# Gate and up projections of four FFNs: one 512 wide product with the high part of a weight block over both parts of the input, then a 256 wide one with its low part

## The chip, the cores and the metric

One core of a Trainium2 chip runs one program. The metric is device time in microseconds (us) from one launch to its end. Engines are named as the profile names them: PE multiplies matrices (PEld is its loading of weights), DVE, ACT and POOL work on tiles in SBUF and PSUM, SP issues most DMAs.

## The reference, cut to what matters

A decoder trunk of two layers over 256 tokens of width 1024, all in float32. Each layer has two half-step FFNs around a token mixer: a gated linear recurrence in the first, attention in the second. So there are four FFNs, and each of them computes

```
def swiglu(x, w_gate, w_up, w_down):            # x 256x1024, w_gate and w_up 1024x2816, w_down 2816x1024
    return (jax.nn.silu(x @ w_gate) * (x @ w_up)) @ w_down
h = h + 0.5 * rms_norm(swiglu(rms_norm(h, g_pre), ...), g_post)
```

The change concerns `x @ w_gate` and `x @ w_up`.

## The kernel before, in words

**Split operands.** PE multiplies in a format that holds fewer bits than float32 (fp32r). So each weight tile `raw` (128 x 1024, 512 KB, loaded by SP) is split: ACT writes the rounded copy `whi` (L175), DVE the rest `wlo = raw - whi` (L176). The normed input is kept in the same way, turned, in `xall` (128 x 8 x 2 x 256): for each of 8 blocks of 128 features, 256 columns of the high part (`xhi`) and right behind them 256 columns of the low part (`xlo`). A product `w * x` is the sum of three: high times high, high times low, low times high.

**Two ways to project.** `mm3` (L181 to L185) keeps a block of the *input* still in PE and streams 512 weight columns; three products per block. `mmj` (L195 to L200) keeps a *weight* block (128 x 128) still and streams 256 tokens:

```
def mmj(ps, wh, wl, k, first, last):
    nc.tensor.matmul(ps, wh, xhi[:, k, :], start=first, stop=False)     # L198
    nc.tensor.matmul(ps, wh, xlo[:, k, :], start=False, stop=False)     # L199
    nc.tensor.matmul(ps, wl, xhi[:, k, :], start=False, stop=last)      # L200
```

The first two use the same weights, but each product loads its own. The result comes out turned (features in partitions, tokens in columns), as the down projection wants its still operand.

**An FFN** (`ffn_items`, L479) covers the 2816 hidden columns in five tiles of 512 and one of 256. The first tile of three of the four FFNs goes by `mm3` (gate, then up), the others by `mmj`: `tile_items` (L535) for 512 columns of the gate, then 512 of up; `last_items` (L558) for 256 of each. Such a *group* is four weight tiles, each with 2 x 4 blocks of 128 x 128, so 32 calls of `mmj`. Over all FFNs these are 38 groups, 152 weight tiles, 1216 calls, 3648 products. A group writes two PSUM banks of 512 columns, two blocks in each. At its end `gate_rows` (L518: DVE scales by the row of reciprocal norms `rrow`, ACT applies SiLU) or `up_rows` (L525: DVE multiplies with the gate, ACT makes `hhi`, DVE `hlo`) reads each of the two banks. Then comes the down projection (`row_items`, L440) by `mm3` with 512 wide products.

**PSUM** has 8 banks. Before, four rotate as `mm` (sums), two as `gt` (turning of the stream `h`), two as `tr` (other transpositions).

**Order.** PE's order is written out by hand: `run_ffn` (L606) goes through the items, `slot` does one item and calls `tick`, and `tick` places small work that was deferred by a number of ticks, such as transpositions (`hidden_T` L506, `rstd_rows` L256, `rg_params` L670, which turns the parameters of the recurrence once, in the first FFN). The other engines' orders come from a scheduler. Raw tiles have 5 buffers (`RAW`), split ones 9 (`WB`); a split is placed by `prepare_next` when its buffer is free and its load is estimated to have landed.

Of the kernel before, what the change touches and what calls it, by code (L numbers as in the profile page):

```python
# [16 lines left out]
P = 128  # L17
# [27 lines left out]
def trunk_kernel(ctx: ExitStack, tc: tile.TileContext, A: dict, out: bass.AP):  # L45
# [12 lines left out]
    def nm(s):  # L58
        uid[0] += 1
        return f"{s}_{uid[0]}"  # L60

    def mmbank():
        return psum.tile([P, 512], F32, tag="mm", name=nm("mm"), bufs=4)

    def gtbank():
        return psum.tile([P, 512], F32, tag="gt", name=nm("gt"), bufs=2)

    def trbank():
        return psum.tile([P, 512], F32, tag="tr", name=nm("tr"), bufs=2)

# [123 lines left out]

    def mmj(ps, wh, wl, k, first, last):  # L195

        tensor_work(3 * S)
        nc.tensor.matmul(ps, wh, xhi[:, k, :], start=first, stop=False)  # L198
        nc.tensor.matmul(ps, wh, xlo[:, k, :], start=False, stop=False)  # L199
        nc.tensor.matmul(ps, wl, xhi[:, k, :], start=False, stop=last)  # L200

# [54 lines left out]
    def rstd_rows():  # L256

        tp = trbank()
# [124 lines left out]
    def proj_items(w, c0, nn, get_x, post, nk=8):  # L383
# [4 lines left out]
        for k0 in range(0, nk, kper):  # L388
# [8 lines left out]
            def work(t, u, k0=k0, kn=kn, i=len(items)):  # L397
# [12 lines left out]
                if k0 + kn == nk:  # L410
                    post(t, acc[t][:, :nn])
            if not items:
# [27 lines left out]
    def row_items(w, widths, get_x, post, rows=2):  # L440
# [6 lines left out]
        for k, kp in enumerate(widths):  # L447
# [3 lines left out]
            def work(t, u, k=k):  # L451
# [13 lines left out]
                if k == nk - 1:  # L465
                    post(t, acc[t])
            items.append((prep, work))
            r0 += kp
# [10 lines left out]
    def ffn_items(pool_of, wg, wu, wd, post_g, next_dests, last=False, normed=False, lead=1):  # L479
# [9 lines left out]

        def gate_tile():  # L490
            return pool_of().tile([P, 512], F32, tag="sil", name=nm("sil"), bufs=2)

        def prod_tile():
            return pool_of().tile([P, 8 * HA], F32, tag="prod", name=nm("prod"), bufs=2)[:, :512]

        def post_gate(t, ps):
            s = sil[t] = gate_tile()
            nc.scalar.activation(s, ps, AF.Silu, scale=rs[t][:, 0:1])

        def post_up(c0):  # L500
            def f(t, ps):
                pr = prod_tile()
                nc.vector.tensor_tensor(pr, ps, sil[t], ALU.mult)
                defer(HT, lambda: hidden_T(pr, t))

            def hidden_T(pr, t):  # L506
                hh, hl = hid_tiles()
                tp = trbank()
                for j in range(4):
                    nc.tensor.transpose(tp[:, j * P:(j + 1) * P], pr[:, j * P:(j + 1) * P], ident)  # L510
                k0 = c0 // P
                hv = hh[:, t, k0:k0 + 4, :].rearrange("p a b -> p (a b)")
                lv = hl[:, t, k0:k0 + 4, :].rearrange("p a b -> p (a b)")
                nc.scalar.activation(hv, tp, AF.Copy)
                nc.vector.tensor_tensor(lv, tp, hv.bitcast(F32), ALU.subtract)
            return f

        def gate_rows(n, ps):  # L518
            s = sil["j", n] = gate_tile()
            v = s.rearrange("p (a b) -> p a b", a=2)  # L520
            nc.vector.tensor_tensor(v, ps.rearrange("p (a b) -> p a b", a=2),
                                    rcp["v"].unsqueeze(1).to_broadcast([P, 2, S]), ALU.mult)
            nc.scalar.activation(s, s, AF.Silu)

        def up_rows(n, ps, k0):  # L525
            hh, hl = hid_tiles()
            pr = prod_tile()
            nc.vector.tensor_tensor(pr, ps, sil["j", n], ALU.mult)
            pv = pr.rearrange("p (a t b) -> p a t b", a=2, t=2)
            hv = hh[:, :, k0:k0 + 2, :].rearrange("p t a b -> p a t b")  # L530
            lv = hl[:, :, k0:k0 + 2, :].rearrange("p t a b -> p a t b")
            nc.scalar.activation(hv, pv, AF.Copy)
            nc.vector.tensor_tensor(lv, pv, hv.bitcast(F32), ALU.subtract)

        def tile_items(w, c0, post):  # L535
            acc = {}

            for k0 in range(0, 8, 2):
                def prep(k0=k0):
# [3 lines left out]
                def work(t, u, k0=k0):  # L543
                    if k0 == 0:
                        acc["b"] = [mmbank(), mmbank()]
                    for j in range(2):
                        for b in range(4):
                            o = j * 512 + b * P
                            mmj(acc["b"][b // 2][:, (b % 2) * S:(b % 2 + 1) * S], u.hi[:, o:o + P], u.lo[:, o:o + P],
                                k0 + j, k0 + j + b % 2 == 0, k0 + j == 7 and b % 2 == 1)  # L550
                        if j == 0:
                            tick()
                    if k0 == 6:
                        for n in range(2):
                            post(n, acc["b"][n])
                items.append((prep, work))

        def last_items(c0):  # L558
            acc = {}

            for k0 in range(0, 8, 2):
# [7 lines left out]
                def work(t, u, k0=k0):  # L569
                    if k0 == 0:  # L570
                        acc["b"] = [mmbank(), mmbank()]
                    for j in range(2):
                        for b in range(4):
                            o = j * 512 + b * P
                            mmj(acc["b"][b // 2][:, (b % 2) * S:(b % 2 + 1) * S], u.hi[:, o:o + P], u.lo[:, o:o + P],
                                k0 + j, k0 + j + b % 2 == 0, k0 + j == 7 and b % 2 == 1)
                        if j == 0:
                            tick()
                    if k0 == 6:
                        gate_rows(0, acc["b"][0])  # L580
                        up_rows(0, acc["b"][1], c0 // P)
                items.append((prep, work))

        i0 = len(items)
        for i in range(5):
# [84 lines left out]
    def rg_params():  # L670
        tp = trbank()
        nc.tensor.transpose(tp[:RT, :NP], prow, ident[:NP, :NP])
# [33 lines left out]
    def add_gate_unit(g, k0, kn):  # L706
# [5 lines left out]
        def work(t, u):  # L712
# [6 lines left out]
            if k0 + kn == 8:  # L719
                if (g, t) not in ((0, 1), (2, 0)):  # L720
                    for gg, tt_ in {(1, 1): [(0, 1)], (2, 1): [(2, 0)]}.get((g, t), []) + [(g, t)]:
                        n = GCOLS[gg][1]
                        tok = toks[(gg, tt_)] = pools["r"].tile([P, 4 * RT], F32, tag="tok", name=nm("tok"), bufs=4)
                        nc.scalar.activation(tok[:, :n], gacc[(gg, tt_)][:, :n], AF.Gelu_apprx_tanh)
        rg[f"g{sum(n[0] == 'g' and n[1] != 'w' for n in rg)}"] = len(items)
        items.append((prep, work))
# [35 lines left out]
    def conv(p, ps):  # L762
# [9 lines left out]
        def taps(j, i):  # L772
            for k in (2, 1, 0):
                s = 3 - k
                nc.vector.scalar_tensor_tensor(xc[:w, j, s:], ps[:w, j * S:(j + 1) * S - s],
                                               par[:w, k * NRT + i:k * NRT + i + 1], xc[:w, j, s:], ALU.mult, ALU.add)

        first = [(1.25, ("c", p), lambda j=j, i=i: taps(j, i)) for j, i in enumerate(tl)]
# [79 lines left out]
    def batch(g):  # L858
# [20 lines left out]
        def gate_T(t):  # L879
            tok = toks[(g, t)]  # L880
            tp = tps[t] = trbank()
            for j in range(len(pairs) * 2 if g < 2 else 3):
# [3 lines left out]
        def product(t):  # L886
# [4 lines left out]
            for (a, b, w) in parts_of(g):  # L891
                tp = tps[t][:w, a * P:b * P].rearrange("p (a b) -> p a b", a=b - a)
                nc.vector.tensor_tensor(y[:w, a:b, :], tp, tt[g][:w, a:b, t * P:(t + 1) * P], ALU.mult)
                nc.scalar.activation(yy[g][0][:w, t, a:b, :], y[:w, a:b, :], AF.Copy)

        def low(t):
# [82 lines left out]
    def heads_T(pool, ps, t, n, scale, cols, dst):  # L979

        tok = pool.tile([P, 8, HA], F32, tag="prod", name=nm("htok"), bufs=2)
        nc.vector.tensor_scalar(tok[:, :, :HD], ps.rearrange("p (a b) -> p a b", a=8), rs[t][:, 0:1], scale,
# [7 lines left out]
        def turn(b):  # L990
            tp = trbank()
            for j in range(4):
# [41 lines left out]
    def v_items(c0, n, extra):  # L1034
# [3 lines left out]
        for k0 in range(0, 8, 2):  # L1038
# [9 lines left out]
            def work(t, u, k0=k0):  # L1048
# [6 lines left out]
                if k0 == 6:  # L1055
                    if extra:
                        post_f(t, ps[:, n:])
                    nc.scalar.activation(kv["v"][t][:, c0:c0 + n], ps[:, :n], AF.Copy, scale=rs[t][:, 0:1])
            items.append((prep, work))

# [20 lines left out]
    def attention(t):  # L1081
# [32 lines left out]
        def values(hg):  # L1114
# [8 lines left out]
            if hds[-1] % 8 == 7:  # L1123
                nc.vector.reciprocal(sm, sm)
                ot = box["ot", hds[-1] // 8] = ap.tile([P, 8, HD], F32, tag="ot", name=nm("ot"), bufs=2)
                nc.vector.tensor_tensor(ot, po.rearrange("p (a b) -> p a b", a=8),
                                        sm.unsqueeze(2).to_broadcast([P, 8, HD]), ALU.mult)

        def output(b):
# [198 lines left out]
```

## Time and profile before

| | before |
|---|---|
| median of 3 runs | 1019.05 us (1018.81 to 1019.17) |
| the profiled execution | 1018.94 us |
| its span, first to last instruction | 1017.2 us |
| PE products, all | 6518 |
| of them 256 wide by `mmj` | 3 x 1216 |
| granted PE clock | 0.998 |

A time is 1.7 us longer than the span of the same execution (1018.94 against 1017.2). Products are pipelined: a product's shown duration includes the time in which it drains, while the next one already streams. So what a product costs in a row of products is the distance from its start to the next one's start, which the timeline shows.

### The profile page before, as it was taken

Reading aid. Unit: us, or ns where it says so; the run is one execution under the profiler, and the core shown is the slowest. Engines: PE = TensorE matmul, PEld = TensorE weight load, DVE = VectorE, ACT = ScalarE, POOL = GpSimd, SP = SyncE. Lnnn points to the kernel's source line nnn. Section 1 sums busy time; section 2 is a strip of 40 time slices with the busy share of each in tenths; the row PEclk is TensorE's granted clock in tenths of the full one; section 3 lists DMA queues with packets and bytes.
Section 4 is the critical chain, followed back from the end, with each engine's and each line's share of the span. In section 5 each row is a group of like instructions: output and inputs, shape, how many; then the busy total and the mean of one; then the engine's idle time right before and its main releaser. Section 6 shows DMA issues by size and latency. Waiting matters only on the chain.

```text
span 1017.2 us, 16436 instructions
## 1 busy us (share of the span) xinstructions
PE 1004.2 (99%) x6518; PEld 915.0 (90%) x6518; DVE 628.3 (62%) x777; ACT 533.9 (52%) x734; POOL 52.7 (5%) x113
## 2 busy tenths in 40 slices
PE   8999999999999999999999999999999999999997
PEld 5999998889988999998898999998888889999885
DVE  5866554668997655554695555654477476556442
ACT  5645434559986544443565444443467565444331
POOL 2500000000003000000110000000020010000000
PEclk9999999999999999999999999999999999999999
DMA  6886646565336766556376666664555067665441
GB/s 231 284 257 198 192 160 187 164 183 151 122 99 226 229 186 186 187 151 180 116 242 221 191 181 180 185 183 164 165 167 166 1 189 247 186 183 182 155 125 41
DMA packets 91875, 179.07 MB, mean 176 GB/s; under 512 B 11790, under 2 KB 31318, under 8 KB 91798
## 3 DMA queue, kind: packets, MB, share of 16 engines
q1 hardware_dynamic: 90550, 176.89, 56.1%
q8 instruction: 51, 0.84, 0.3%
q10 hardware_dynamic: 608, 1.06, 0.3%
q0 software_dynamic: 640, 0.07, 0.1%
q14 instruction: 26, 0.21, 0.1%
HBM read 176.95 MB, written 1.05 MB: 175 GB/s over the span
## 4 chain that ended last, share of the span: by engine, by line
PE 90%; ACT 4%; DVE 4%; issue 2%; POOL 1%; DVEq 0%; POOLq 0%; ACTq 0%
PE mm L198 14%; PE mm L200 14%; PE mm L199 14%; PE mm L185 13%; PE mm L184 13%; PE mm L183 13%; PE gt L815 1%; DVE wlo L176 1%; PE mm L190 1%; PE mm L191 1%; PE mm L192 1%; PE gt L1094 1%; PE mm L1121 1%; ACT junk L213 1%; PE gt L222 1%
## 5 line engine op out<-in xcount | busy, mean ns | idle before, releaser
L176 DVE TENSOR_TENSOR wlo<-raw,whi 128x1024 fp32r<-128x1024 f32 (+4 forms) x329 | 395.1, 1207 | 297.2 <-ACT whi L175 295.4
L175 ACT ACTIVATE whi<-raw 128x1024 fp32r<-128x1024 f32 (+4 forms) x329 | 342.6, 1046 | 373.8 <-PE mm L199 207.9
L198 PE MATMUL mm<-xall,whi 128*128 128x256 f32 x1216 | 344.7, 283 | 0.0
L200 PE MATMUL mm<-xall,wlo 128*128 128x256 f32 x1216 | 344.1, 283 | 0.0
L199 PE MATMUL mm<-xall,whi 128*128 128x256 f32 x1216 | 344.1, 283 | 0.0
L198 PEld LDWEIGHTS mm<-xall,whi 128*128 128x128 f32 x1216 | 233.4, 192 | 0.2
L199 PEld LDWEIGHTS mm<-xall,whi 128*128 128x128 f32 x1216 | 233.4, 192 | 0.2
L200 PEld LDWEIGHTS mm<-xall,wlo 128*128 128x128 f32 x1216 | 233.4, 192 | 0.0
L183 PE MATMUL mm<-whi,hhi 128*128 128x512 f32 (+2 forms) x432 | 166.1, 384 | 0.0
L185 PE MATMUL mm<-whi,hlo 128*128 128x512 f32 (+2 forms) x432 | 165.0, 382 | 0.0
L184 PE MATMUL mm<-wlo,hhi 128*128 128x512 f32 (+2 forms) x432 | 164.9, 382 | 0.0
L185 PEld LDWEIGHTS mm<-whi,hlo 128*128 128x128 f32 x432 | 81.1, 188 | 15.0
L184 PEld LDWEIGHTS mm<-wlo,hhi 128*128 128x128 f32 x432 | 81.2, 188 | 14.7
L183 PEld LDWEIGHTS mm<-whi,hhi 128*128 128x128 f32 x432 | 81.2, 188 | 14.6
L183 PE MATMUL mm<-whi,xall 128*128 128x512 f32 (+2 forms) x168 | 67.1, 400 | 0.1
L184 PE MATMUL mm<-wlo,xall 128*128 128x512 f32 (+2 forms) x168 | 65.0, 387 | 0.4 <-DVE wlo L1191 0.2
L185 PE MATMUL mm<-whi,xall 128*128 128x512 f32 (+2 forms) x168 | 64.8, 386 | 0.1
L206 POOL TENSOR_SCALAR nv<-ss 128x1 f32<-128x1 f32 x24 | 10.9, 453 | 789.7 <-ACT junk L213 789.5
L184 PEld LDWEIGHTS mm<-wlo,xall 128*128 128x128 f32 x168 | 31.7, 188 | 7.4 <-DVE wlo L176 1.2
L185 PEld LDWEIGHTS mm<-whi,xall 128*128 128x128 f32 x168 | 31.6, 188 | 7.0 <-DVE xall L236 1.1
L183 PEld LDWEIGHTS mm<-whi,xall 128*128 128x128 f32 x168 | 31.6, 188 | 5.7 <-ACT xall L231 0.5
L277 DVE SCALAR_TENSOR_TENSOR t<-mm,rstd,gb 128x512 f32<-128x512 f32 x16 | 11.9, 749 | 26.7 <-ACT junk L213 26.7
(188 smaller groups left out, 938.9 us busy)
## 6 DMA issues: line engine op xcount, KB each, us to landing
raw<-in_ffn_w_down_dram SPq DMA_DIRECT2D x88, 512.0 KB
raw<-in_ffn_w_up_dram SPq DMA_DIRECT2D x80, 512.0 KB
raw<-in_ffn_w_gate_dram SPq DMA_DIRECT2D x79, 512.0 KB
raw<-in_rg_w_in_dram SPq DMA_DIRECT2D x20, 504.0 KB
raw<-in_rg_w_out_dram SPq DMA_DIRECT2D x10, 504.0 KB
raw<-in_ffn_w_gate_dram SPq DMA_DIRECT2D x18, 256.0 KB
raw<-in_ffn_w_up_dram SPq DMA_DIRECT2D x16, 256.0 KB
raw<-in_w_kv_dram SPq DMA_DIRECT2D x8, 512.0 KB
```

The costliest lines, as they stand in the source:

```text
L175: nc.scalar.activation(hi[:parts, c:c + m], rawv[:, c:c + m], AF.Copy)
L176: nc.vector.tensor_tensor(lo[:parts, c:c + m], rawv[:, c:c + m], hi[:parts, c:c + m].bitcast(F32), ALU.subtract)
L183: nc.tensor.matmul(ps, xh, wh, start=first, stop=False)
L184: nc.tensor.matmul(ps, xh, wl, start=False, stop=False)
L185: nc.tensor.matmul(ps, xl, wh, start=False, stop=last)
L190: nc.tensor.matmul(ps, wh, xh, start=first, stop=False)
L191: nc.tensor.matmul(ps, wh, xl, start=False, stop=False)
L198: nc.tensor.matmul(ps, wh, xhi[:, k, :], start=first, stop=False)
L199: nc.tensor.matmul(ps, wh, xlo[:, k, :], start=False, stop=False)
L200: nc.tensor.matmul(ps, wl, xhi[:, k, :], start=False, stop=last)
L206: nc.gpsimd.tensor_scalar(v, ss[:, 0:1], ss[:, 1:2] if n == 2 else 0.0, D * EPS * f * f, ALU.add, ALU.add)
L277: nc.vector.scalar_tensor_tensor(t1[n], pf[n], r_in, gb[:, n * 512:(n + 1) * 512], ALU.mult, ALU.mult)
```

## The change

`mmj` now takes two neighbouring blocks. For each it issues one 512 wide product of `wh` with both input parts, which lie side by side in `xall`, and after both of these the two 256 wide products of `wl` with the high part. The sums high times high and low times high stand in columns 0 to 255 of a bank, high times low in columns 256 to 511. So each block has a bank of its own, and a group four banks instead of two; the two halves are added when the bank is read out (`total`: ACT copies the second halves of all banks of a group to SBUF, DVE adds the first halves).

All 8 banks become one tile `pall`, handed out by `bank`. Gate groups and `last_items` use banks 4 to 7, up groups banks 0 to 3; while banks are in such use (`lent`), the small transpositions take one of the others (`sparebank`). `gate_rows` and `up_rows` do a whole group (1024 columns) in one instruction where there were two of 512, and their buffers `sil` and `prod` become one tile of 1024 instead of two of 512. After the sum, `gate_rows` scales and `up_rows` multiplies in an instruction of their own.

```diff
-    def mmj(ps, wh, wl, k, first, last):
-
-        tensor_work(3 * S)
-        nc.tensor.matmul(ps, wh, xhi[:, k, :], start=first, stop=False)
-        nc.tensor.matmul(ps, wh, xlo[:, k, :], start=False, stop=False)
-        nc.tensor.matmul(ps, wl, xhi[:, k, :], start=False, stop=last)
+    def mmj(bs, wh, wl, k):
+
+        tensor_work(3 * S * len(bs))
+        for b, w in zip(bs, wh):
+            nc.tensor.matmul(pall[:, b, :], w, xall[:, k, :, :].rearrange("p a b -> p (a b)"), start=k == 0, stop=False)
+        for b, w in zip(bs, wl):
+            nc.tensor.matmul(pall[:, b, :S], w, xhi[:, k, :], start=False, stop=k == 7)
...
-        def gate_rows(n, ps):
-            s = sil["j", n] = gate_tile()
-            v = s.rearrange("p (a b) -> p a b", a=2)
-            nc.vector.tensor_tensor(v, ps.rearrange("p (a b) -> p a b", a=2),
-                                    rcp["v"].unsqueeze(1).to_broadcast([P, 2, S]), ALU.mult)
+        def total(v, b, m):
+
+            nc.scalar.activation(v, pall[:, b:b + m, S:], AF.Copy)
+            nc.vector.tensor_tensor(v, pall[:, b:b + m, :S], v, ALU.add)
+
+        def gate_rows(b, m):
+            s = sil["j"] = gate_tile(m * S)
+            v = s.rearrange("p (a b) -> p a b", a=m)
+            total(v, b, m)
+            nc.vector.tensor_tensor(v, v, rcp["v"].unsqueeze(1).to_broadcast([P, m, S]), ALU.mult)
             nc.scalar.activation(s, s, AF.Silu)
 
-        def up_rows(n, ps, k0):
+        def up_rows(b, m, k0):
             hh, hl = hid_tiles()
-            pr = prod_tile()
-            nc.vector.tensor_tensor(pr, ps, sil["j", n], ALU.mult)
...
+            pr = prod_tile(m * S)
+            total(pr.rearrange("p (a b) -> p a b", a=m), b, m)
+            nc.vector.tensor_tensor(pr, pr, sil["j"], ALU.mult)
...
+        def still(t, u, k0, b0):
+            if k0 == 0:
+                assert not set(held) & set(range(b0, b0 + 4)), held.keys()
+                lent.update(range(b0, b0 + 4))
+            for j in range(2):
+                for b in range(0, 4, 2):
+                    os = [j * 512 + (b + i) * P for i in range(2)]
+                    mmj([b0 + b, b0 + b + 1], [u.hi[:, o:o + P] for o in os], [u.lo[:, o:o + P] for o in os], k0 + j)
+                if j == 0:
+                    tick()
+            if k0 == 6:
+                lent.difference_update(range(b0, b0 + 4))
...
-                tile_items(wg, i * 512, gate_rows)
-                tile_items(wu, i * 512, lambda n, ps, i=i: up_rows(n, ps, 4 * i + 2 * n))
+                tile_items(wg, i * 512, 4, gate_rows)
+                tile_items(wu, i * 512, 0, lambda b, m, i=i: up_rows(b, m, 4 * i))
...
     def rg_params():
-        tp = trbank()
+        tp = sparebank()
```

More of the change, by code (lines that the diff above doesn't have):

```diff
@@ L501, in f @@
             def f(t, ps):
-                pr = prod_tile()
+                if t == 0:
+                    box["p"] = prod_tile(1024)
+                pr = box["p"][:, t * 512:(t + 1) * 512]
                 nc.vector.tensor_tensor(pr, ps, sil[t], ALU.mult)
@@ L569, in work @@
                 def work(t, u, k0=k0):
[L570 to L578, printed above, removed]
+                    still(t, u, k0, 4)
                     if k0 == 6:
-                        gate_rows(0, acc["b"][0])
-                        up_rows(0, acc["b"][1], c0 // P)
+                        gate_rows(4, 2)
+                        up_rows(6, 2, c0 // P)
                 items.append((prep, work))
```

85 lines of the change are left out of this document (52 added, 33 removed).

## The prediction

> **What bounds the kernel now.** I read the page's first, second and fourth parts, then the costliest groups.
>
> ```profile
> span 1017.2 us, 16436 instructions
> PE 1004.2 (99%) x6518; PEld 915.0 (90%) x6518; DVE 628.3 (62%) x777; ACT 533.9 (52%) x734; POOL 52.7 (5%) x113
> PE   8999999999999999999999999999999999999997
> PEclk9999999999999999999999999999999999999999
> PE 90%; ACT 4%; DVE 4%; issue 2%; POOL 1%; DVEq 0%; POOLq 0%; ACTq 0%
> L198 PE MATMUL mm<-xall,whi 128*128 128x256 f32 x1216 | 344.7, 283 | 0.0
> L200 PE MATMUL mm<-xall,wlo 128*128 128x256 f32 x1216 | 344.1, 283 | 0.0
> L199 PE MATMUL mm<-xall,whi 128*128 128x256 f32 x1216 | 344.1, 283 | 0.0
> ```
>
> PE works in every slice at full clock, and the chain that ended last is PE for 90%. The three rows of `mmj` have no idle time ahead of them. Their 283 ns cannot be the price of a product, since 3 x 1216 x 283 ns would be 1033 us, more than the whole span; products overlap. The price is the distance between starts, read from the timeline inside a gate group of the first FFN:
>
> ```profile
> 119.87 0.28 PE L198 MATMUL mm<-xall,whi 128*128 128x256 f32 x1
> 119.99 0.28 PE L199 MATMUL mm<-xall,whi 128*128 128x256 f32 x1
> ...
> 123.47 0.28 PE L198 MATMUL mm<-xall,whi 128*128 128x256 f32 x1
> ```
>
> From 119.87 to 123.47 lie ten blocks of three products: 3.60 us / 30 = 120 ns. So `mmj` costs 360 ns, and 1216 calls 437.8 us, 43% of the span. Can anything else end last in these stages? The windows of such stretches of the first two FFNs (columns: us, then PE, PEld, DVE, ACT, POOL busy) and two rows of the waits say no:
>
> ```profile
> 48.00:140.00 92.00, 92.00 (x769) 92.00 (x768) 57.08 (x77) 45.22 (x52) 0.00 (x0) 1.00 0.69 215
> 344.00:444.00 100.00, 100.00 (x836) 100.00 (x835) 59.01 (x61) 44.91 (x52) 0.11 (x1) 1.00 0.64 193
> DVE wlo L176 <- ACT whi L175: 295.4, 231, 3.7
> ACT whi L175 <- PE mm L199: 207.9, 123, 1.9
> ```
>
> DVE is busy 62% and 59%, ACT 49% and 45%, the DMA engines two thirds. ACT waits 207.9 us for PE to give a split buffer back (L199 is the last reader of `whi`), and DVE waits for ACT: the weights stand ready ahead of PE, not the other way. So in these stretches PE's own products are the bound, and only fewer or cheaper products shorten them.
>
> **The change, part by part.** *Products removed.* Per block three starts become two, and the streamed columns stay 768. What a 512 wide product of this number format costs, also with a new weight block each time, is seen in the down projection:
>
> ```profile
> 145.18 0.39 PE L183 MATMUL mm<-whi,hhi 128*128 128x512 f32 x1
> 145.40 0.39 PE L184 MATMUL mm<-wlo,hhi 128*128 128x512 f32 x1
> ...
> 185.97 0.39 PE L183 MATMUL mm<-whi,hhi 128*128 128x512 f32 x1
> ```
>
> Sixty blocks of three lie between: 40.79 us / 180 = 226.6 ns. So 256 more columns cost 106.6 ns and the first 256 cost 120: a start has a price of its own, 13.4 ns, whatever it streams. If every product in the new mix cost what it costs among its like, a pair of blocks would go from 6 x 120 = 720 to 2 x 226.6 + 2 x 120 = 693.2 ns.
>
> But the mix is new: two wide, two narrow, in turn. The trace has both switches, each deep inside a stream of its kind. From narrow to wide, where a down projection begins:
>
> ```profile
> 140.27 0.28 PE L200 MATMUL mm<-xall,wlo 128*128 128x256 f32 x1
> 140.39 0.40 PE L183 MATMUL mm<-whi,hhi 128*128 128x512 f32 x1
> 140.62 0.40 PE L184 MATMUL mm<-wlo,hhi 128*128 128x512 f32 x1
> 140.86 0.39 PE L185 MATMUL mm<-whi,hlo 128*128 128x512 f32 x1
> ...
> 141.55 0.39 PE L185 MATMUL mm<-whi,hlo 128*128 128x512 f32 x1
> 141.78 0.39 PE L183 MATMUL mm<-whi,hhi 128*128 128x512 f32 x1
> ```
>
> The first two wide products take 140.39 to 140.86, 470 ns, where two settled ones take 453; the first five take 1160 against 1133; the sixth is settled. And from wide to narrow:
>
> ```profile
> 340.06 0.28 PE L198 MATMUL mm<-xall,whi 128*128 128x256 f32 x1
> 340.17 0.28 PE L199 MATMUL mm<-xall,whi 128*128 128x256 f32 x1
> 340.29 0.28 PE L200 MATMUL mm<-xall,wlo 128*128 128x256 f32 x1
> 340.41 0.28 PE L198 MATMUL mm<-xall,whi 128*128 128x256 f32 x1
> ```
>
> The first two take 340.06 to 340.29, 230 ns, a little under 240. In the change every pair begins with narrow to wide and has wide to narrow in its middle, so I take these two rows as they stand: 470 + 232 (the 230 is rounded to 10 ns; 232 lies between it and 2 x 120, near to it) = 702 ns per pair. That is 18 ns less than 720, and for 608 pairs **10.9 us less**. The bounds: each place at its lowest row (wide 226.6, narrow 115) gives 683, 22.5 us less; each at its highest (235, 120) gives 710, 6.1 us less.
>
> By the Trainium skill, "TensorE: Matmul & The Clock Gate", section "Back-to-back issue gap", a warm product costs its columns at 2.4 GHz and about 2.5 ns, so a removed start would be worth 2.5 ns and all 1216 of them 3.0 us. The trace agrees with the share of the columns (106.6 ns for 256) and not with the fixed part (13.4 ns here, for fp32r with a new weight block each time).
>
> *Read-out added.* Durations of what is there now, by shapes:
>
> ```profile
> L176 DVE TENSOR_TENSOR wlo<-raw,whi 128x1024 fp32r<-128x1024 f32 x284 | 345.9, 1224 | 284.4 <-ACT whi L175 282.6 <-DMA gw<-in_rg_w_x_dram 0.9 <-issue 0.3
> L175 ACT ACTIVATE whi<-raw 128x1024 fp32r<-128x1024 f32 x284 | 300.0, 1059 | 356.1 <-PE mm L199 207.9 <-PE mm L185 121.1 <-ACT hhi L532 12.6
> L528 DVE TENSOR_TENSOR prod<-mm,sil 128x512 f32<-128x512 f32 x38 | 26.2, 690 | 0.5
> L521 DVE TENSOR_TENSOR sil<-mm,rrow 128x512 f32<-128x512 f32 x38 | 26.1, 690 | 0.7 <-PE mm L200 0.2
> L533 DVE TENSOR_TENSOR hlo<-prod,hhi 128x512 fp32r<-128x512 f32 x38 | 24.6, 686 | 2.8 <-ACT hhi L532 2.8
> L532 ACT ACTIVATE hhi<-prod 128x512 fp32r<-128x512 f32 x38 | 21.8, 617 | 5.5 <-DVE prod L528 5.5
> ```
>
> For a gate and an up group together DVE had six instructions of about 690 ns (4.1 us) and gets five of 1024 columns: two sums, the scaling, the product, the low part, 5 x 1.22 = 6.1 us. ACT had four of 617 (2.5) and gets four of 1.06 (4.2). A 1024 wide read of PSUM is in no row; from 690 at 512 and 1224 at 1024 from SBUF I take 1.2, and were it twice 690 it would be 1.4. So DVE gains 2.0 us and ACT 1.8 per two groups, which last 2 x 32 x 351 ns = 22.5 us: DVE goes from 62% to about 71%, ACT to 57%. Both stay beside PE, and **cost nothing**: the weights are nine buffers ahead. If that cover were gone, 19 x 2.0 = 38 us would show.
>
> *Banks.* A group now holds four banks until ACT's copy and DVE's sum are done: 1.06 + 1.22 = 2.3 us, 4.6 with a split in front of each. Gate and up groups alternate between two sets of four, so a set rests for a whole group, 11.2 us. In the built order of the changed kernel the first product of a group waits for the sum of the last group on the same banks, and for no other. Cover 6.6 us; cost nothing. The transpositions that now borrow a bank are the exception. One of them, `rg_params`, runs once:
>
> ```profile
> L672 PE MATMUL tr<-ident,prow x1: 240/240/240, 84.1 to 84.1; 88*126 88x88 f32 x1
> ```
>
> Before, it had a `tr` bank to itself. In the changed order it stands eight products (1.4 us) behind the end of an up group and writes one of that group's banks, so it waits for copy and sum. PE is in order, and all products of the next group queue behind it. Copy and sum need 2.3 us, 3.4 with a split in front, so PE stands 0.9 to 2.0 us; I take **1.5 us more**. The first gate groups of an FFN begin on banks that transpositions used before; these were read 2.6 us earlier or more (0.6 us of ACT and 0.7 of DVE), and I count nothing.
>
> *Loads.* 512 KB per item come 2.5% oftener, at 220 GB/s in the first window and 198 in the second against the 322 that a stretch at 60 us shows:
>
> ```profile
> 60.00:65.00 5.00, 5.00 (x44) 5.00 (x43) 4.19 (x5) 2.93 (x4) 0.00 (x0) 1.00 0.98 322
> ```
>
> That is no bound. All other stages keep their products.
>
> *Sum:* -10.9 + 1.5 = -9.4 us. The profiled execution took 1018.94, so 1009.5; the median shown, 1019.05, is 0.1 above it, and so I predict **1009.6 us**.
>
> **The rivals.** *The mix settles.* Both streams, left alone, fall into their cheap rhythm after five products; the new pattern repeats every four and may find one too. Then a pair is 693.2 ns, 16.3 us less, and the time 1019.05 - 16.3 + 1.5 = 1004.3. Against it: no row shows such a mix settled. *It never settles and narrow gains nothing*: 470 + 240 = 710, 6.1 us less, 1014.5. For it: the narrow products may be cheap only behind a settled wide one. *Better than both*: 683, 22.5 us less, 998; it needs the wide settled and the narrow unsettled at once, which speaks against it.
>
> *Slower.* A switch of kind can be dearer than the rows above. Behind transpositions the first wide product stands out:
>
> ```profile
> 310.84 0.48 PE L183 MATMUL mm<-whi,y 126*128 126x512 f32 x1
> 311.15 0.40 PE L184 MATMUL mm<-wlo,y 126*128 126x512 f32 x1
> ```
>
> 310 ns, 83 above a settled one. If each pair paid that once, it would be 702 - 235 + 310 = 777, 57 more than now, and the time 1019.05 + 34.7 + 1.5 = 1055. It decides from a pair of 717.5 ns on, where the 2.5 ns per pair of the `rg_params` wait are eaten up. Against it: these transpositions are of another number format, and the two switches inside one format, above, show nothing of it.
>
> *A start is nearly free.* If most of the 13.4 ns followed the columns and not the start, a wide product would approach 2 x 120 = 240 and only a remainder of each start would go: with wide at 237, a pair is 714, 3.6 us less, 1016.9 with the wait. The 226.6 speaks against it. The rule of the Trainium skill named above gives about this, 1019.05 - 3.0 + 1.5 = 1017.6.
>
> **How the numbers follow.** Chances: forecast 0.45, settled 0.25, unsettled 0.15, better than both 0.05, start nearly free 0.05, slower 0.05. The range leaves out the last three (0.15): from settled with the short wait, 1003.6, to unsettled with the long one, 1015.0, each with a margin of about 1 us for what the stalls at the ends of the stages do: **1003 to 1016**. A difference of 0.2%, about 2 us, is what a measurement of this kernel can tell from none. All cases but the last two are faster by more: faster 0.90. "Start nearly free" lies at the bound: same 0.05. Slower 0.05.
>
> **What the profile of the changed kernel would show.** 2 x 1216 rows of `mmj` products, half of them 512 wide; inside a group, a distance of 702 ns from the first wide product of a pair to that of the next (693 settled, 710 unsettled, over 717 slower), and within it 235, 235, 113 and 119. DVE about 71% busy in such a stretch, ACT 57%, and no idle time of PE at the first product of a group. One wait of PE of 0.9 to 2.0 us for DVE's sum, at the transposition of `rg_params`. Wrong would be: idle PE at group starts (banks), PE waiting for DVE's `wlo` in these stretches (DVE the bound), or a distance that isn't the same all through.

## The result, and the profile after

The changed kernel takes **1008.55 us** (median of 4 runs, 1006.91 to 1008.93); before took 1019.11 beside it (1018.81 to 1019.47). The ratio is 0.9893, 95% interval 0.9876 to 0.991. The profiled execution took 1008.27 us with a span of 1006.6, 10.6 less than before's 1017.2. First the rows of the page that answer to those of before:

```profile
span 1006.6 us, 13910 instructions
PE 991.9 (99%) x5302; PEld 847.9 (84%) x5302; DVE 665.6 (66%) x768; ACT 566.0 (56%) x742; POOL 51.5 (5%) x113
L223 PE MATMUL pall<-xall,whi 128*128 128x512 f32 x1216 | 382.5, 396 | 0.0
L225 PE MATMUL pall<-xall,wlo 128*128 128x256 f32 x1216 | 239.0, 278 | 0.0
```

1216 products fewer (5302 against 6518), half of `mmj`'s 512 wide, and PE is still 99% busy. Where the time went is read from the distances between starts. The timeline of PE through the second FFN's gate and up projections, after (start, duration of the whole group of x2, engine, line):

```profile
340.25 0.61 PE L223 MATMUL pall<-xall,whi 128*128 128x512 f32 x2
...
399.92 0.63 PE L223 MATMUL pall<-xall,whi 128*128 128x512 f32 x2
...
405.49 0.40 PE L223 MATMUL pall<-xall,whi 128*128 128x512 f32 x1
...
441.02 0.40 PE L207 MATMUL pall<-whi,hhi 128*128 128x512 f32 x1
```

and three rows of the same view of before: the turning of the input, the first `mmj` product, and the first product of the second FFN's down projection:

```profile
5.25 0.97 PE L222 MATMUL gt<-ident,h 128*128 128x128 f32 x4
...
35.81 0.28 PE L198 MATMUL mm<-xall,whi 128*128 128x256 f32 x1
...
444.15 0.40 PE L183 MATMUL mm<-whi,hhi 128*128 128x512 f32 x1
```

From 399.92 to 405.49 lie eight pairs of blocks: 5.57 / 8 = 696 ns a pair, against 720 before and 702 forecast. From the first product to the down projection the second stage takes 441.02 - 340.25 = 100.77 us after and 444.15 - 340.06 = 104.09 before: 3.32 us less, and it holds 9 groups, 144 pairs, so 23.1 ns less per pair. All starts of the four stages, counted in the same way (the first one without the wait told below), give 3.27, 3.32, 4.05 and 3.34 us: **14.0 us less** for 608 pairs, 23.0 each, a pair of 697.0 on the mean. Between disturbances (the transpositions within a stage) a pair takes 696.7 ns in each of the four stages.

Two things take part of that back. A row of PE's waits, after (total in us, times, longest), and the stretch around it (ACT, DVE and PE, with the idle time and its releaser in brackets):

```profile
PE pall L701 <- issue: 2.0, 1, 2.0
```

```profile
82.53 1.06 ACT L199 ACTIVATE whi<-raw 128x1024 fp32r<-128x1024 f32 x1 [1.73 <-PE pall L223]
83.49 1.00 ACT L551 ACTIVATE prod<-pall 128x1024 f32<-128x1024 f32 x1
83.62 1.23 DVE L200 TENSOR_TENSOR wlo<-raw,whi 128x1024 fp32r<-128x1024 f32 x1 [1.56 <-ACT whi L199]
83.67 0.39 PE L225 MATMUL pall<-xall,wlo 128*128 128x256 f32 x2
84.76 1.22 DVE L552 TENSOR_TENSOR prod<-pall,prod 128x1024 f32<-128x1024 f32 x1
86.08 0.27 PE L701 MATMUL pall<-ident,prow 88*126 88x88 f32 x1 [2.02 <-issue]
86.14 0.70 PE L223 MATMUL pall<-xall,whi 128*128 128x512 f32 x2
```

L701 is `rg_params`. The product before it began at 83.79 (the second of the two at 83.67) and it begins at 86.08: 2.29 us, **2.17 more** than the usual 0.12. The profile names no releaser ("issue"), but DVE's sum L552 ends at 85.98, 0.1 us before. That sum began late because of two splits. The group's last product was followed by the next group's first at 82.51, but ACT's copy L551 began only at 83.49, behind a split on ACT (`whi`, L199). And when the copy ended at 84.49, another split (`wlo`, L200) stood in front of the sum on DVE, which cost 0.3 us more. No row of L223 is among the waits: no group waits for its banks. The other wait is at the very start:

```profile
6.34 0.90 PE L247 MATMUL pall<-ident,h 128*128 128x128 f32 x3 [1.01 <-DMA h<-in_x_dram]
...
37.08 0.62 PE L223 MATMUL pall<-xall,whi 128*128 128x512 f32 x2
```

The turning of the input begins at 6.34 against 5.25 before, and the first `mmj` product 37.08 against 35.81, **1.3 us** later. The change doesn't touch that stage. In the other kernels below that leave it alone too, the first `mmj` product starts between 35.84 and 36.56; so most of this term belongs to this one execution. The span, then: -14.0 + 2.2 + 1.3 = -10.5, and the stages between, 0.13 shorter in sum: -10.6, the difference of the two spans.

The windows of the two stretches (us; PE, PEld, DVE, ACT, POOL busy; clock, DMA share, GB/s) show the engines beside PE:

```profile
48.00:140.00 92.00, 89.98 (x518) 78.41 (x517) 65.77 (x73) 51.72 (x52) 0.00 (x0) 1.00 0.69 218
344.00:444.00 100.00, 100.00 (x573) 87.14 (x572) 68.92 (x60) 54.14 (x56) 0.00 (x0) 1.00 0.64 198
```

DVE is busy 71% and 69%, ACT 56% and 54%; the 2.0 us that PE lacks in the first window are the wait.

### The profile page after: what moved, and what is told of

It reads as the page before. It is cut to its first block, busy times and chain, and to the rows that moved or that the text cites. A ratio compares the mean times of both kernels' runs of the same rounds, so it can differ in the third digit from the quotient of the medians.

```text
span 1006.6 us, 13910 instructions
## 1 busy us (share of the span) xinstructions
PE 991.9 (99%) x5302; PEld 847.9 (84%) x5302; DVE 665.6 (66%) x768; ACT 566.0 (56%) x742; POOL 51.5 (5%) x113
## 4 chain that ended last, share of the span: by engine, by line
PE 70%; issue 20%; ACT 4%; DVE 4%; POOL 1%; DMA 1%; DVEq 0%; POOLq 0%; ACTq 0%
PE pall L223 21%; PE pall L225 11%; PE pall L209 10%; PE pall L208 10%; PE pall L207 10%; PE pall L847 1%; DVE wlo L200 1%; PE pall L214 1%; PE pall L215 1%; PE pall L216 1%; PE pall L1130 1%; ACT junk L238 1%; PE pall L1157 1%; ACT whi L199 1%; PE pall L1028 1%
## 5 line engine op out<-in xcount | busy, mean ns | idle before, releaser
L200 DVE TENSOR_TENSOR wlo<-raw,whi 128x1024 fp32r<-128x1024 f32 (+4 forms) x329 | 394.7, 1206 | 240.7 <-ACT whi L199 240.1
L199 ACT ACTIVATE whi<-raw 128x1024 fp32r<-128x1024 f32 (+4 forms) x329 | 342.0, 1044 | 287.8 <-PE pall L209 125.3
L223 PE MATMUL pall<-xall,whi 128*128 128x512 f32 x1216 | 382.5, 396 | 0.0
L225 PEld LDWEIGHTS pall<-xall,wlo 128*128 128x128 f32 x1216 | 228.4, 188 | 54.0
L225 PE MATMUL pall<-xall,wlo 128*128 128x256 f32 x1216 | 239.0, 278 | 0.0
L223 PEld LDWEIGHTS pall<-xall,whi 128*128 128x128 f32 x1216 | 185.5, 189 | 0.4
L207 PE MATMUL pall<-whi,hhi 128*128 128x512 f32 (+2 forms) x432 | 166.0, 384 | 0.0
L209 PE MATMUL pall<-whi,hlo 128*128 128x512 f32 (+2 forms) x432 | 164.9, 382 | 0.0
L208 PE MATMUL pall<-wlo,hhi 128*128 128x512 f32 (+2 forms) x432 | 164.9, 382 | 0.0
L208 PEld LDWEIGHTS pall<-wlo,hhi 128*128 128x128 f32 x432 | 81.2, 188 | 14.6
L207 PEld LDWEIGHTS pall<-whi,hhi 128*128 128x128 f32 x432 | 81.2, 188 | 14.5
L207 PE MATMUL pall<-whi,xall 128*128 128x512 f32 (+2 forms) x168 | 67.2, 400 | 0.1
L209 PE MATMUL pall<-whi,xall 128*128 128x512 f32 (+2 forms) x168 | 64.9, 386 | 0.1
```

Source lines behind the costliest of these rows:

```text
L199: nc.scalar.activation(hi[:parts, c:c + m], rawv[:, c:c + m], AF.Copy)
L200: nc.vector.tensor_tensor(lo[:parts, c:c + m], rawv[:, c:c + m], hi[:parts, c:c + m].bitcast(F32), ALU.subtract)
L207: nc.tensor.matmul(ps, xh, wh, start=first, stop=False)
L208: nc.tensor.matmul(ps, xh, wl, start=False, stop=False)
L209: nc.tensor.matmul(ps, xl, wh, start=False, stop=last)
L223: nc.tensor.matmul(pall[:, b, :], w, xall[:, k, :, :].rearrange("p a b -> p (a b)"), start=k == 0, stop=False)
```

## The experiments

The theory: PE's stream is the bound; a start has a price of its own, the read-out and the banks are hidden, and a change between wide and narrow products gives part of the saving back. The rivals are named with each run. All times stand against before, 1019.33, 1019.18 and 1019.26 us in the three batches.

**1. Is the whole gain the start that is left out?** Everything of the change stays (banks, sums, read-out); only the wide product is cut in two again.

```diff
-            nc.tensor.matmul(pall[:, b, :], w, xall[:, k, :, :].rearrange("p a b -> p (a b)"), start=k == 0, stop=False)
+            nc.tensor.matmul(pall[:, b, :S], w, xhi[:, k, :], start=k == 0, stop=False)
+            nc.tensor.matmul(pall[:, b, S:], w, xlo[:, k, :], start=False, stop=False)
```

> The changed kernel with each wide product cut again into two of 256 columns, on the same bank halves; banks, read-out and all else as in the changed kernel. If the whole gain is the missing start, 1216 products of 256 cost 120 each again: the stage products take 360 ns a block as before, and the time is that of before plus the one wait of the recurrence's parameters (2.2 us in the profile of the changed kernel), 1021.2, plus up to 1.1 if the input lands late as it did there. If banks or read-out had brought part of the gain, it would lie under 1018; if they cost something, over 1023.

Measured: 1021.38 us (8 runs, 1021.18 to 1023.09), ratio 1.0023 (1.0013 to 1.0034). Its timeline of PE:

```profile
400.30 0.28 PE L223 MATMUL pall<-xall,whi 128*128 128x256 f32 x1
400.42 0.28 PE L224 MATMUL pall<-xall,whi 128*128 128x256 f32 x1
...
405.34 0.28 PE L223 MATMUL pall<-xall,whi 128*128 128x256 f32 x1
```

Seven pairs in 5.04 us: 720 again. The second to fourth stages are as long as before's, to 0.01 us, so banks and read-out bring nothing and cost nothing there. The gain is gone, and what remains, 2.05 us over before, is about the wait at `rg_params`. So the 1216 starts alone carry the gain: 1021.38 - 1008.55 = 12.8 us, 10.6 ns each. A start is here a product together with its own load of weights; no run parts the two, so which of them has the price stays open. By the rule of the Trainium skill that the prediction weighed ("TensorE: Matmul & The Clock Gate", "Back-to-back issue gap", 2.5 ns a start, given there for an isolated product) it would be an estimated 3.0 us; the trace doesn't agree.

**2. Is it the operands or the company that makes the wide product 233 ns instead of 227?** The low part's product becomes 512 wide too; this adds low times low, which the other kernels leave out.

```diff
-        for b, w in zip(bs, wh):
-            nc.tensor.matmul(pall[:, b, :], w, xall[:, k, :, :].rearrange("p a b -> p (a b)"), start=k == 0, stop=False)
-        for b, w in zip(bs, wl):
-            nc.tensor.matmul(pall[:, b, :S], w, xhi[:, k, :], start=False, stop=k == 7)
+        for b, w in list(zip(bs, wh)) + list(zip(bs, wl)):
+            nc.tensor.matmul(pall[:, b, :], w, xall[:, k, :, :].rearrange("p a b -> p (a b)"),
+                             start=k == 0 and any(w is v for v in wh), stop=k == 7 and any(w is v for v in wl))
```

> The changed kernel with the low weights' product made 512 wide too: it adds low times low to the upper half of the bank, a term that the kernels leave out. All products of the stage are then 512 wide and none 256. Theory mixed company: the wide products cost 233.5 only because narrow ones stand between them; among wide ones alone they cost 226.6, a pair 906.4 ns, and the time is 1008.5 + 608 x (906.4 - 697.7) = 1135. Theory operands: 233.5 is the price of a 512 wide product on these operands (input streamed, one bank whole per block); then a pair is 934 ns and the time 1152.

Measured, one run: 1134.65 us.

```profile
400.40 0.62 PE L223 MATMUL pall<-xall,whi 128*128 128x512 f32 x2
...
404.94 0.39 PE L223 MATMUL pall<-xall,whi 128*128 128x512 f32 x1
```

Twenty products in 4.54 us: 227.0 each, with these operands and these banks. So it is the company of narrow products that costs 6 ns per wide one.

**3. Is the read-out hidden?** DVE doubles and halves each sum once more, two more instructions of 1024 columns per read-out.

```diff
             nc.vector.tensor_tensor(v, pall[:, b:b + m, :S], v, ALU.add)
+            nc.vector.tensor_tensor(v, v, v, ALU.add)
+            nc.vector.tensor_scalar(v, v, 0.5, None, ALU.mult)
```

> The changed kernel with two more instructions of 1024 columns on DVE in each read-out (the sum doubled and halved again; it changes no value). DVE is busy 69 to 71% of these stages in the changed kernel and would come to about 80 to 90%. If the read-out is hidden, the time stays, about 1008.5 (up to 2 more at the one wait of the parameters, which then waits for nothing new: the sum itself is not later). If DVE were near to being the bound, or PE waited for splits behind it, 38 x 2 us or a part would show: over 1015.

Measured: 1008.74 us (1008.5 to 1008.9), ratio 0.9896 (0.988 to 0.9913), the time of the change itself. A window of it:

```profile
344.00:444.00 100.00, 100.00 (x573) 87.23 (x572) 82.42 (x75) 53.99 (x55) 0.00 (x0) 1.00 0.64 198
```

DVE is 82% busy and PE doesn't notice; the second to fourth stages have the length they have after, to 0.01 us. The first is 1.6 us longer, by the half clock behind the wait at `rg_params` (last section); in this execution an earlier start of the first stage makes up for most of that.

**4. Are the two sets of banks what hides it?** Up groups use the same four banks as gate groups.

```diff
-                tile_items(wu, i * 512, 0, lambda b, m, i=i: up_rows(b, m, 4 * i))
+                tile_items(wu, i * 512, 4, lambda b, m, i=i: up_rows(b, m, 4 * i))
```

> The changed kernel with up groups on banks 4 to 7 as well, so that each group follows on banks that the one before it has just filled. It takes away the rest of 11.2 us that the two sets give the read-out. Of 38 groups 34 follow another at once. If the read-out lies beside PE only because of the two sets, PE stands at each of these for the drain, ACT's copy, DVE's sum and what is queued ahead of them, 2.5 to 3.6 us (3.6 is what the parameters' transposition needed from the end of its group in the changed kernel): 85 to 122 us more, 1094 to 1131. Rival: the read-out is hidden in another way (each bank freed by itself, PE working ahead), and the time rises by under 20.

Measured, one run: 1167.46 us, above the expected 1094 to 1131. The window and the start of one group on PE:

```profile
48.00:140.00 92.00, 72.94 (x371) 62.39 (x370) 49.01 (x58) 39.30 (x39) 0.00 (x0) 0.91 0.54 165
```

```profile
67.04 1.05 PE L223 MATMUL pall<-xall,whi 128*128 128x512 f32 x2
...
68.32 1.05 PE L223 MATMUL pall<-xall,whi 128*128 128x512 f32 x2
...
77.87 0.40 PE L225 MATMUL pall<-xall,wlo 128*128 128x256 f32 x2
81.62 0.72 PE L223 MATMUL pall<-xall,whi 128*128 128x512 f32 x2 [3.36 <-DVE sil L552]
```

Now the first product of a group waits 3.36 us for DVE's sum: the second set is what makes the read-out free. The 34 waits sum to 113 us, which lies within the expected 85 to 122. The rest is the clock: behind 23 of the waits it was granted at half for a while, 92 us in all (0.91 on the mean of the window), and a pair then took 68.32 - 67.04 = 1.28 us instead of 0.70. Half of these 92 us, an estimated 46, is lost; with the waits that makes up the 159 us over the change. The expectation had only the wait.

**5. What is the wait at `rg_params` worth?** It is placed six ticks later, away from the end of an up group.

```diff
-    defer(40, rg_params)
+    defer(46, rg_params)
```

> The changed kernel with the transposition of the recurrence's parameters put six ticks later, near the end of the next gate group, when the sum of the banks that it borrows is long done. If PE's wait of 2.2 us there is what it seems, it goes and nothing is late in its place: about 1006.4. Rival: the parameters' later arithmetic or ACT's table load then holds up something else, and the time stays about 1008.5 or rises.

Measured: **1005.3 us** (1004.99 to 1005.69), ratio 0.9862 (0.9846 to 0.9879).

```profile
91.40 0.39 PE L225 MATMUL pall<-xall,wlo 128*128 128x256 f32 x2
91.63 0.24 PE L701 MATMUL pall<-ident,prow 88*126 88x88 f32 x1
```

The transposition starts at its place, with no wait, and the first stage is 2.19 us shorter. This is the version that beats both kernels, 3.25 us under the change. The wait is 2.2 of that; between the two profiled executions (1008.27 and 1005.42, 2.85 apart) the other 0.63 is the earlier start of the first `mmj` product, 36.45 against 37.08. The rest of the 3.25 may be the clock of the runs without a profile (last section), which isn't shown.

**6. The order of wide and narrow.** Three kernels change only the order: in turn, four and four, eight and eight.

```diff
-        for b, w in zip(bs, wh):
+        for b, w, v in zip(bs, wh, wl):
...
-        for b, w in zip(bs, wl):
-            nc.tensor.matmul(pall[:, b, :S], w, xhi[:, k, :], start=False, stop=k == 7)
+            nc.tensor.matmul(pall[:, b, :S], v, xhi[:, k, :], start=False, stop=k == 7)
```

> The changed kernel, but each block's wide product is followed at once by its own narrow one (wide, narrow, wide, narrow). In the changed kernel a pair of blocks takes about 698 ns: the wide products 233.9 and 233.2 on average, the narrow ones 114.7 and 115.9; settled among their like they would be 226.6 and 120. Theory A (place after a switch): what counts is how many products of its kind ran just before, by the rows of before: first wide 233, second 236, first narrow 113.5, second 119. Then a pair is 2 x (233 + 113.5) = 693 ns, 2.9 us less than the changed kernel: about 1005.6. Theory B (price of a switch): each change from narrow to wide and back costs what a pair is over 693.2, 4.6 ns; twice as many changes make 702.4 ns a pair, 2.8 us more than the changed kernel: about 1011.4. Theory C: the order doesn't matter, 698 ns and about 1008.5.

> The changed kernel with four blocks in place of two: four wide products, then four narrow ones, so half as many changes of kind. Theory A (place after a switch): 233 + 236 + 228 + 233 and 113.5 + 119 + 120 + 120, 1402.5 ns for four blocks, 701 a pair, 2.1 us more than the changed kernel: about 1010.6. Theory B (price of a switch): half the 4.6 ns, 695.5 a pair, 1.4 us less: about 1007.1. Theory C: the order doesn't matter, about 1008.5.

> The changed kernel with eight wide products (four blocks, both row blocks of a weight tile) and then the eight narrow ones. Orders so far: 1 and 1 gave 699.0 ns a pair of blocks, 2 and 2 697.7, 4 and 4 702.0. Theory A (place after a switch, as in before): the wide ones 233, 236, 228, 233, 231 and three of 227, the narrow ones 113.5, 119 and six of 120: 2795 for eight blocks, 699 a pair, about 1009. Theory D (a mix never settles, and long runs have dear wide products and no cheap narrow ones): wide 233, narrow 119.5: 705, about 1013.

For four and four, `mmj` gets all four blocks of a k step at once:

```diff
-                for b in range(0, 4, 2):
-                    os = [j * 512 + (b + i) * P for i in range(2)]
-                    mmj([b0 + b, b0 + b + 1], [u.hi[:, o:o + P] for o in os], [u.lo[:, o:o + P] for o in os], k0 + j)
+                os = [j * 512 + b * P for b in range(4)]
+                mmj([b0 + b for b in range(4)], [u.hi[:, o:o + P] for o in os], [u.lo[:, o:o + P] for o in os], k0 + j)
```

Eight and eight issues the wide products of both k steps of a weight tile and then all narrow ones. Measured: in turn 1008.86 us (1007.0 to 1009.99), ratio 0.9895 (0.9881 to 0.991); fours 1009.99 (1009.72 to 1010.48), 0.9909 (0.9894 to 0.9924); eights, one run, 1007.15. The timeline of PE with fours, and with eights:

```profile
400.63 1.09 PE L223 MATMUL pall<-xall,whi 128*128 128x512 f32 x4
401.56 0.64 PE L225 MATMUL pall<-xall,wlo 128*128 128x256 f32 x4
...
404.83 0.39 PE L223 MATMUL pall<-xall,whi 128*128 128x512 f32 x1
```

```profile
400.29 2.00 PE L223 MATMUL pall<-xall,whi 128*128 128x512 f32 x8
402.13 1.12 PE L225 MATMUL pall<-xall,wlo 128*128 128x256 f32 x8
403.08 2.00 PE L223 MATMUL pall<-xall,whi 128*128 128x512 f32 x8
```

Fours take 4.20 / 6 = 700 ns a pair in this second stage, and about 701.5 in the three other stages; eights take 2.79 / 4 = 698 here and 698.4 over all starts between disturbances. The prices by the place behind a switch, read from the two switches of before, had 701 and 699. With eights they hold place by place (wide 233.5, 236, 228, 232, 231, then 227; narrow 113.6, 119, then 120). With fours only the sum fits: in the second stage the wide ones cost 230, 231, 236 and 228, the narrow ones 117, 118, 119 and 121. Theory B's 695.5 with fours doesn't fit, nor its 702.4 in turn, nor Theory C's 698 with fours. And for products in turn the prices by the place had 693, while the mean between disturbances is 697.8 (the 699.0 and 702.0 named above count the slow starts behind transpositions too). That mean hides two things, seen in two windows of that kernel, one late in the first stage and one in the second:

```profile
124.88 0.39 PE L223 MATMUL pall<-xall,whi 128*128 128x512 f32 x1
...
130.77 0.39 PE L223 MATMUL pall<-xall,whi 128*128 128x512 f32 x1
...
399.88 0.40 PE L223 MATMUL pall<-xall,whi 128*128 128x512 f32 x1
...
405.89 0.40 PE L223 MATMUL pall<-xall,whi 128*128 128x512 f32 x1
```

Seventeen blocks take 5.89 us in the first of these and 6.01 in the second: 693 and 707 ns a pair. Over all starts between the disturbances it is 693.3 or 706.6, steady over each undisturbed stretch. In the slow rhythm six products repeat: wide 232, narrow 118, wide 241, narrow 120, wide 236, narrow 114. So the price of a product isn't fixed by its place behind the switch; it has a memory over several pairs.

**7. What picks the rhythm?** Products in turn once more without a change, and products in turn with `rg_params` six ticks later. (The letters of these two expectations are theories of their own.)

> The kernel with wide and narrow products in turn once more, unchanged. Theory D: the program fixes what stands ahead of each stage, so the rhythms come back as they were: 706.6 ns per pair before the wait in the first stage and in the second stage, 693.3 behind the wait, in the third and the fourth. Rival F: the rhythm falls anew in each execution: at least one stage changes from 706.6 to 693.3 or back. The time is 1007 to 1010 us by both.

> Wide and narrow products in turn, and the turning of the parameters six ticks later. In the first run with products in turn a pair of blocks took 706.6 ns in the first stage up to the wait at 83 us and in the whole second stage, and 693.3 ns behind that wait, in the third and in the fourth stage. Theory D: products in turn have two lasting rhythms, and what stands ahead of a stage (or a long wait inside it) picks one. Then without the wait the first stage keeps 706.6 to its end: 288 pairs at 706.6 and 320 at 693.3, 1.8 us more than two wide and two narrow at 696.7 each, so 1005.3 + 1.8 = 1007.1 us. Rival E: the order settles at 693.3 sooner or later by itself, as it did by chance at 83 us: the first stage ends at 693.3 too, 1003 to 1005 us.

Measured: again, one run, 1007.82 us; with `rg_params` later 1005.77 (1005.66 to 1006.01), ratio 0.9869 (0.9852 to 0.9885). In all three executions the second stage runs at 706.6 and the third and fourth at 693.3. But the first differs, here the same stretch of it, in the first execution and in the second:

```profile
59.61 0.40 PE L223 MATMUL pall<-xall,whi 128*128 128x512 f32 x1
...
65.97 0.40 PE L223 MATMUL pall<-xall,whi 128*128 128x512 f32 x1
```

```profile
59.95 0.39 PE L223 MATMUL pall<-xall,whi 128*128 128x512 f32 x1
...
65.85 0.39 PE L223 MATMUL pall<-xall,whi 128*128 128x512 f32 x1
```

Eighteen blocks in 6.36 us (707 a pair) against seventeen in 5.90 (694). So Theory D, by which the program fixes the rhythm, fails for the first stage. With `rg_params` later, the rhythm changes exactly there, though nothing waits:

```profile
83.63 0.40 PE L223 MATMUL pall<-xall,whi 128*128 128x512 f32 x1
...
89.99 0.40 PE L223 MATMUL pall<-xall,whi 128*128 128x512 f32 x1
...
91.75 0.24 PE L700 MATMUL pall<-ident,prow 88*126 88x88 f32 x1
...
93.94 0.39 PE L223 MATMUL pall<-xall,whi 128*128 128x512 f32 x1
...
99.83 0.40 PE L223 MATMUL pall<-xall,whi 128*128 128x512 f32 x1
```

Eighteen blocks in 6.36 before the transposition (707 a pair), seventeen in 5.89 behind it (693). The only two changes of rhythm that the three traces show inside a stage lie at this transposition (in the first execution with the wait, here without); in the second execution it changed nothing, and the other changes lie between stages. In an undisturbed stretch there is none, and the second stage keeps 706.6 to its end. So a disturbance can change the rhythm without the wait of D, and E's settling by itself isn't seen; the time, 1005.77, lies between D's 1007.1 and E's 1005; which rhythm a given disturbance picks, and what in PE keeps it, stays open. Two and two, as in the change, showed one rhythm only, 696.7, in all four stages, here and with `rg_params` later. In turn is therefore no gain over it: 1005.77 against 1005.3.

## Why the prediction was right, point by point

- **PE's stream is the bound, and a start has a price of its own.** Right: shown by experiment 1, in which the gain goes with the starts and all else of the change stays. The price of 13.4 ns among products of one width came to 14.0 us / 1216 = 11.5 ns in the mix.
- **A pair of blocks: 702 forecast, 697.0 measured.** The mechanism was right (a switch costs something, in between 693.2 and 710), the size of this term 3.0 us off in 608 pairs. The measured pair lies nearer to the rival "settled" (693.2) than to the forecast. The term took the four places of the switches as they stand, 235, 235, 113, 119. Over a stretch of the second stage (43 pairs between 400 and 430 us) they are 233, 233, 115 and 116: the first narrow product is dearer, the second cheaper, and both wide ones a little cheaper. The two switches of before come out of settled streams and the change's never do; experiments 6 and 7 show that what went before counts over several pairs.
- **Read-out at no cost.** Right: DVE 69% to 71%, ACT 54% to 56%, and experiment 3 puts two more instructions of the same size into each read-out, and three stages keep their length.
- **Banks at no cost.** Right in the change; experiment 4 shows what it hangs on. The expectation of that experiment was right on the waits and left out the clock.
- **The wait at `rg_params`: 1.5 forecast (0.9 to 2.0), 2.17 measured.** Right in place and cause, too short: the case with a split in front came true, on ACT in front of the copy and for 0.3 us on DVE in front of the sum, and it came out 0.2 above its own upper bound; 0.1 of that passes between the end of the sum and the start on PE. Experiment 5 takes it away.
- **Loads no bound, all other stages as they were.** Right for the stages between (0.13 us in all). Not foreseen was the input's landing, 1.1 us later in this execution; the kernels below turn the input in the same way and start `mmj` 0.5 to 1.2 us earlier, so most of this isn't the change's.
- **The sum.** -14.0 + 2.2 + 1.3 against -10.9 + 1.5: three terms 3.1 less, 0.7 more and 1.3 more, so that 1008.27 stood 1.2 us below the 1009.5 worked out for the profiled execution. That the errors cancel so nearly is luck. Without the late input the working with the measured terms gives 1019.05 - 14.0 + 2.2 - 0.1 = 1007.1, 2.5 under the forecast; one of the four runs took 1006.91.
- **The rivals.** "Settled" (693.2) doesn't hold for two and two; products in turn reach its sum in one of their rhythms, but by other prices (230 and 117, or 232 and 115, where it has 226.6 and 120); "never settles" (710), "slower" (777 a pair), "better than both" (683) and "start nearly free" (714) are refuted by the 697.0. The 310 ns behind a transposition, on which "slower" leaned, comes once behind each transposition and not in each pair.

## What to carry to other kernels

Where PE is the bound, take the price of a product from start to start and split it into columns and start: here 1216 left out starts, 13.4 ns each among products of one width, were worth 14.0 us in the mix, with more work on DVE and ACT that PE waited for only once. A mix of widths costs neither the sum of the settled prices nor that of the switches, so measure the order that will run, between two disturbances and in each stage by itself. And look for the one small instruction that loses its own buffer by the change: moving it six ticks took away its wait of 2.2 us.

## What the runs showed of the hardware that was not expected

**A short wait of PE can halve the clock; where it falls decides.** In all twelve traces the granted clock, once full, changes only at whole multiples of 3.41 us, counted from where it first became full. These intervals lie elsewhere in each execution. Here are two intervals around the wait at `rg_params` in experiment 3, and then two in the change (columns as above; the clock stands after the five engines):

```profile
82.74:86.15 3.41, 1.39 (x9) 1.10 (x9) 3.38 (x4) 0.65 (x1) 0.00 (x0) 1.00 0.78 219
86.15:89.56 3.41, 3.41 (x13) 2.92 (x12) 3.38 (x8) 2.93 (x5) 0.00 (x0) 0.50 0.43 120
```

```profile
81.60:85.01 3.41, 2.46 (x15) 2.00 (x13) 1.85 (x3) 1.97 (x2) 0.00 (x0) 1.00 0.81 252
85.01:88.43 3.42, 2.35 (x14) 2.12 (x15) 2.60 (x5) 1.16 (x3) 0.00 (x0) 1.00 0.67 194
```

In experiment 3 the wait lies inside one interval, in which PE is idle for 2.02 us, and the next interval runs at half clock. In the change the same wait is cut by the end of an interval, 0.95 us in one and 1.07 in the next, and the clock stays full. Over all traces, each of the 24 intervals at full clock with 1.96 us of idle PE or more was followed by half clock, and none with 1.87 or less; of three with 1.89 to 1.90 one was. That also sorts the waits of experiment 4: one of 3.36 us, halved by the end of an interval, leaves the clock full.

An interval at half clock costs an estimated 1.7 us, half of its 3.41; the first stage of experiment 3 is 1.6 us longer. Experiment 1 shows it in its runs: five with a mean clock of 0.999 took 1021.18 to 1021.46 us, three with 0.997 took 1022.44 to 1023.09. The runs of the change with 0.998 took 1006.91 and 1008.27 us, those with 0.996 and 0.997 took 1008.93 and 1008.82, which fits, though only one of them has a trace. The Trainium skill ("TensorE: Matmul & The Clock Gate", "HAM oscillation — how this bites in real kernels") tells of idle gaps above about 3.4 us that bring the half clock; in these runs 1.96 us were enough inside one interval, and 11 waits of 2.4 to 3.4 us in experiment 4 went without it.

**Mixed widths fall into a lasting rhythm**: products in turn in one of two, 693.3 or 706.6 ns a pair, and at a single small transposition, with no wait, PE went from the one to the other. Four and four show two as well, 700.0 in the second stage and about 701.5 in the others.
